# A fused decoder layer on one core: the output projection by pairs of token blocks

## The chip, the cores and the metric

The kernel runs on one core of a Trainium2 chip. The metric is device time in microseconds (us) of one execution. The engines are TensorE (PE, with its weight loads shown apart as PEld), VectorE (DVE), ScalarE (ACT), GpSimd (POOL) and SyncE (SP), which issues the DMAs here.

## The reference, cut to what matters

One decoder layer over 2048 tokens with 1024 channels, all in float32. The input goes through RMSNorm and one input projection into two token mixers of 512 channels each, an S5 scan with GLU and an RG-LRU. Their outputs are normalised, concatenated, projected and added to the residual; then come a SwiGLU feed-forward block and a last RMSNorm.

```python
s5_out  = s5_mixer(u, ...)        # ends in: z = gelu(y); z = z * sigmoid(z @ w_glu + b_glu)
lru_out = rglru_mixer(xr, yr, ...)
mix = concatenate([rms_norm(s5_out, s5_out_g), rms_norm(lru_out, lru_out_g)], axis=-1)
x = x + mix @ w_out               # the output projection, 1024 x 1024
h2 = rms_norm(x, norm2_g)
x = x + (silu(h2 @ w_gate) * (h2 @ w_up)) @ w_down
return rms_norm(x, final_g)
```

The change concerns the GLU and the line with `w_out`, and by its place the start of the gate/up stage that follows.

## The kernel before, in words

Channels lie on the 128 partitions and tokens on the free axis. The 2048 tokens are four blocks of TB = 512 (NB = 4), so that a product fills one PSUM bank (128 x 512 in float32).

**Matrix products in three parts.** Every float32 operand is split into a high part, rounded to the fast float32 format, and a low part, the rest. `mm3` (L193) does three matmuls for each 128 x 128 piece of weights: high x high, high x low, low x high. `Unit` (L168) loads a group of weights in parts of four pieces: the load into `wraw` (L181, six buffers), the cast to `whi` on ScalarE (L187, four buffers) and the subtraction to `wlo` on VectorE or GpSimd (L188, four buffers). A group of the output projection (128 output channels, eight pieces) is two such parts, and takes 24 matmuls for a block of tokens.

**The stages around the change.** `in_tb` (L593) does the input projection and the RG-LRU of one block. The S5 scan runs in two halves of the tokens (L840, blocks 0 and 1, then 2 and 3), eight steps each; its second half runs beside the GLU and the projection of the first two blocks. `glu_tb` (L859) does the GLU of a block: it loads z (L866, `zload`) and the RG-LRU output (`lload`), applies GELU, splits z (`zsplit`, L884), multiplies with `w_glu` (96 matmuls for two blocks), applies the sigmoid and the product (L908), sums squares, and `finish` (L242) makes the factor `rs`. `mix` (L914) then norms each of eight chunks: `norm_split` (L280) does nf on VectorE (L282), the cast (L283) and the subtraction on VectorE or GpSimd (L284). The result goes to `pair(b)` (L856): the pieces aH and aL for blocks 0 and 2, the tiles actH and actL for blocks 1 and 3. `out_tb` (L924) does the projection of a block: for each of eight groups m of weights the 24 matmuls into one of two banks named acc (L142), the addition of the residual (L940, `xc`), the square and its sum, and the store to `x1d` (L942). `finish` then writes the factor of the second RMSNorm to `r2d`.

**The gate/up stage behind it.** `x_first` (L1055) prepares its operands for blocks 0 and 1 in four steps of one chunk k: two loads of `x1d` and one of `r2d` into three tiles `hx` (L1025, L1027), the norm (L1031), sums of the blocks (L1039 to L1042, into four tiles `ht`), and the splits to xh and xl (L995, L996). Each product (L1156) sums over all four chunks. `weights` (L1095) loads and combines the weights.

**Memory.** `open_d1` (L969) closes the pools of the earlier stages (sQ with aH and aL, sL, sS) and opens the pool of the gate/up stage over them. A tile waits for the last reader of what lay there before. In the compiled kernel before, the three hx lie over aH and aL (bytes 47,712 to 60,000 of each partition: aH chunks 0 to 3, aL chunks 4 and 5), the four ht over aH chunks 4 to 7, and the xh and xl of chunk 0 of three products over the rest of aL; the others lie over the pools sL and sS.

**Order.** Each step is put into a plan with a due time (`at`, L64), counted from PT = 0.65 for each piece of weights. The steps are emitted by due time; the compiler then orders each engine's instructions by a simulated schedule in which the emitted order is the priority and an instruction whose inputs or tiles are not ready lets later ones pass. The order of the stages is a list: GLU of 1, projection of 0, projection of 1, GLU of 2, GLU of 3, projection of 2, projection of 3 (L953; GLU of 0 stands in the input stage, L951). tC is the planned end of the projection; `open_d1` is due at tC - 64 PT + 4 and `x_first` at tC - 64 PT + 12 (L1404, L1406), which is the planned begin of block 3's projection.

Of the kernel before, what the change touches and what calls it, by code (L numbers as in the profile page):

```python
# [17 lines left out]
SEQ, DM, TB = 2048, 1024, 512  # L18
NB = SEQ // TB
# [8 lines left out]
PT = 0.65  # L28
# [31 lines left out]
class Plan:  # L60
# [3 lines left out]
    def at(self, t, fn):  # L64
        self.ev.append((t, len(self.ev), fn))
# [14 lines left out]
def build(tc, nc, I, O, ctx):  # L80
    pl = Plan()
    at = pl.at
    PE, DV, AC, GP, SP = nc.tensor, nc.vector, nc.scalar, nc.gpsimd, nc.sync
# [33 lines left out]
    def dram(name, shape):  # L117
        return tc.dram_tile(list(shape), F32, name=name)
# [7 lines left out]
    r2d = dram("r2d", (SEQ,))  # L126
# [6 lines left out]
    xT, out = I["xT"], O  # L133
# [8 lines left out]
    def acc():  # L142
        return PS.tile([128, TB], F32, tag="acc", name="acc", bufs=2)

    last = {}

    def act(**kw):

        ins = AC.activation(**kw)
        ins = getattr(ins, "ins", ins)  # L150
        if "i" in last:
            tc.add_manual_dep(ins, last["i"].name, NOSYNC, reason="tables")
        last["i"] = ins

    def aux(tag, bufs=1):
        return PS.tile([128, TB], F32, tag=tag, name=tag, bufs=bufs)

    def t2(tag, pool=None):
        return (pool or A).tile([128, TB], F32, tag=tag, name=tag, bufs=2)

    def tp():
        return S["p"]

    def r_(ap):
        return ap.bitcast(R)
# [35 lines left out]
    def chunks_of(t):  # L201
        return lambda k: t[:, k, :]
# [67 lines left out]
    def load_chunk(src, b, k, pool=A, tag="xc", bufs=4):  # L270
        t = pool.tile([128, TB], F32, tag=tag, name=tag, bufs=bufs)
        SP.dma_start(t, src[k * 128:(k + 1) * 128, b * TB:(b + 1) * TB])
        return t
# [292 lines left out]
    def lt(tag, shape=(128, 2, TB), dt=F32, bufs=1):  # L566
        return pL.tile(list(shape), dt, tag=tag, name=tag, bufs=bufs)
# [157 lines left out]
    T = 0.0  # L725
    tin = []
    for b in range(NB):
        tin.append(T)
        T = in_tb(b, T)
# [11 lines left out]
    def bt(tag, shape=(128, 2, NS), bufs=1):  # L741
        return S["p"].tile(list(shape), F32, tag=tag, name=tag, bufs=bufs)
# [109 lines left out]
    C = {}  # L852

    t2s = tP1 + 1.0

    def pair(b):  # L856
        return (areaH, areaL) if b % 2 == 0 else (chunks_of(actH), chunks_of(actL))

    def glu_tb(b, t0):  # L859
        cur = C[b] = {}  # L860

        def zload():
            z = cur["z"] = S["z"] if b % 2 == 0 else lt("wg", (128, 4, TB))
            o = CB * (b % 2)
            for j in range(4):
                SP.dma_start(z[:, j].rearrange("p (t c) -> p t c", t=CT),  # L866
                             zb[b // 2, :, 8 * j:8 * j + 8, :, o:o + CB].rearrange("t g h c -> (g h) t c"))

        def lload():
            cur["rl"] = lt("xq", (128, TB))  # L870
            cur["l"] = [lt("r", bufs=2) for _ in range(2)]
            SP.dma_start(cur["rl"], rld[b].unsqueeze(0).to_broadcast([128, TB]))
            for h in range(2):
                SP.dma_start(cur["l"][h], lrud[256 * h:256 * h + 256, b * TB:(b + 1) * TB].rearrange("(j p) t -> p j t", j=2))

        def zgelu():
            act(out=cur["z"], in_=cur["z"], func=AF.Gelu_apprx_tanh)

        def zsplit():
            zh, zl = pair(b)  # L880
            z = cur["z"]
            for j in range(4):
                AC.copy(r_(zh(j)), z[:, j, :])
                DV.tensor_tensor(out=r_(zl(j)), in0=z[:, j, :], in1=zh(j), op=ALU.subtract)  # L884

        at(tin[3] + 35.0 if b < 2 else t0 - 12.0, zload)
        at(max(t0 - 1.5, tin[3] + 50.0), lload)
        at(tin[3] + 36.5 + 0.1 * b if b < 2 else t0 - 5.0, zgelu)
        at(t0 - 5.0 if b == 0 else max(t0 - 5.0, t2s), zsplit)
        cur["ss"] = SumSq(4, "sumg", 2)  # L890
        for uu in range(2):
            t = t0 + uu * 8 * PT
            u = Unit(t, I["w_glu"][uu], 8, GP if uu else DV)

            def prod(uu=uu, u=u):
                for i in range(2):
                    cur["ps", 2 * uu + i] = acc()
                    mm3(cur["ps", 2 * uu + i], u, [(4 * i + k, k) for k in range(4)],
                        *pair(b), True, True)

            at(t, prod)

            def post(uu=uu):
                for i in range(2):
                    m = 2 * uu + i
                    sg = t2("sg", tp())
                    act(out=sg, in_=cur.pop(("ps", m)), func=AF.Sigmoid, bias=pc("bglu", m))
                    DV.tensor_tensor(out=cur["z"][:, m, :], in0=sg, in1=cur["z"][:, m, :], op=ALU.mult)  # L908
                    cur["ss"].add(cur["z"][:, m, :])

            at(t + 8 * PT + 0.5, post)
        t = t0 + 16 * PT

        def mix(k):  # L914
            src, rs = (cur["z"][:, k, :], cur["rs"]) if k < 4 else (cur["l"][k // 2 - 2][:, k % 2, :], cur["rl"])
            norm_split(k, src, pc("gm", k), rs, *pair(b), eng=GP if k % 2 else DV)

        for i, k in enumerate((4, 5, 6, 7)):
            at(max(t0 + 6.0, t2s) + 0.5 * i, lambda k=k: mix(k))
        at(t + 6.0, lambda: cur.__setitem__("rs", cur["ss"].finish()))  # L920
        for k in range(4):
            at(t + 7.0 + 0.5 * k, lambda k=k: mix(k))

    def out_tb(b, t0):  # L924
        cur = C[b]
        ss = SumSq(8, dv=b == NB - 1)
        for m in range(8):
            t = t0 + m * 8 * PT
            u = Unit(t, I["w_out"][m], 8, GP if m % 3 == 1 else DV)

            def prod(m=m, u=u):
                cur["o", m] = acc()
                mm3(cur["o", m], u, [(k, k) for k in range(8)], *pair(b), True, True)

            at(t - 5, lambda m=m: cur.__setitem__(("x", m), load_chunk(xT, b, m)))
            at(t, prod)

            def post(m=m):
                xc = cur.pop(("x", m))
                DV.tensor_tensor(out=xc, in0=cur.pop(("o", m)), in1=xc, op=ALU.add)  # L940
                ss.add(xc)
                SP.dma_start(x1d[128 * m:128 * m + 128, b * TB:(b + 1) * TB], xc)  # L942

            at(t + 8 * PT + 0.5, post)

        def fin():
            ss.finish(r2d[b * TB:(b + 1) * TB])

        at(t0 + 64 * PT + 4.0, fin)

    glu_tb(0, tin[3] + 64 * PT + 5.3)  # L951
    T = tP1 + 16 * PT
    for kind, b in (("g", 1), ("o", 0), ("o", 1), ("g", 2), ("g", 3), ("o", 2), ("o", 3)):  # L953
        if kind == "g":
            glu_tb(b, T)
            T += 16 * PT
        else:
            out_tb(b, T)
            T += 64 * PT
    tC = T  # L960


# [431 lines left out]
    T = tC  # L1394
    gt = {}
# [103 lines left out]
```

## Time and profile before

| | |
|---|---|
| Median of 3 runs | 2208.16 us (2206.6 to 2210.63) |
| Profiled execution | 2207.93 us, span 2206.2 us |
| Instructions | 26,290 |
| Mean granted TensorE clock | 0.949 |
| Matmuls | 8,632 |
| Packets of the main DMA queue | 251,616; 384.69 MB |

The span runs from the first to the last instruction. Busy times of PE come from pipelined matmuls and can overlap, so idle time is read from windows and waits. A wait is put down to what came last before it. "<-" stands between what is written and what is read, or between who waits and whom it waits for; names are those of the program, with L and the line.

### The profile page before, as it was taken

Reading aid. Unit: us, or ns where it says so; the run is one execution under the profiler, and the core shown is the slowest. Engines: PE = TensorE matmul, PEld = TensorE weight load, DVE = VectorE, ACT = ScalarE, POOL = GpSimd, SP = SyncE. Lnnn points to the kernel's source line nnn. Section 1 sums busy time; section 2 is a strip of 40 time slices with the busy share of each in tenths; the row PEclk is TensorE's granted clock in tenths of the full one; section 3 lists DMA queues with packets and bytes.
Section 4 is the critical chain, followed back from the end, with each engine's and each line's share of the span. In section 5 each row is a group of like instructions: output and inputs, shape, how many; then the busy total and the mean of one; then the engine's idle time right before and its main releaser. Section 6 shows DMA issues by size and latency. Waiting matters only on the chain.

```text
span 2206.2 us, 26290 instructions
## 1 busy us (share of the span) xinstructions
PE 1988.3 (90%) x8632; PEld 1582.2 (72%) x8632; DVE 1335.3 (61%) x1975; ACT 812.1 (37%) x1336; POOL 1114.2 (51%) x904
## 2 busy tenths in 40 slices
PE   7668888878988978799999989999999999999996
PEld 5546666656766856577777767777777788888885
DVE  9998868759957397444444474444444535554744
ACT  4433644364344333223233253233232333333331
POOL 3768556649755377654554561231322326644442
PEclk9868999989898988899999999999999999999998
DMA  6244795573763687744444474443443568854733
GB/s 203 86 130 135 196 224 163 180 174 122 234 203 110 206 276 243 257 154 151 149 155 142 151 254 138 134 148 125 145 137 125 171 214 316 301 163 144 247 101 100
DMA packets 251754, 386.37 MB, mean 175 GB/s; under 512 B 59328, under 2 KB 81120, under 8 KB 251616
## 3 DMA queue, kind: packets, MB, share of 16 engines
q1 hardware_dynamic: 251616, 384.69, 55.5%
q8 instruction: 68, 1.11, 0.2%
q14 instruction: 70, 0.57, 0.1%
HBM read 267.92 MB, written 116.67 MB: 174 GB/s over the span
## 4 chain that ended last, share of the span: by engine, by line
PE 63%; DVE 16%; DMA 8%; POOL 5%; issue 4%; ACT 2%; SPq 1%; POOLq 0%; DVEq 0%; ACTq 0%
PE acc L1156 9%; PE gt L1156 9%; PE y L1156 9%; PE acc L198 6%; PE y L1296 5%; PE v L1156 5%; PE acc L1296 5%; PE gt L1296 5%; PE nm L1156 4%; PE nm L1296 2%; PE v L1296 2%; DVE wlo L188 2%; POOL s_s L824 2%; DMA xq<-xT 2%; DVE xh L633 1%
## 5 line engine op out<-in xcount | busy, mean ns | idle before, releaser
L1169 POOL TENSOR_TENSOR t<-t 128x512 f32<-128x512 f32 x66 | 100.6, 1525 | 343.8 <-DVE t L1195 242.2
L198 PE MATMUL acc<-actH,whi 128*128 128x512 f32 x528 | 219.5, 418 | 55.6 <-DVE gy L682 14.0
L995 ACT CAST whi<-ws 128x512 fp32r<-128x512 f32 x176 | 109.1, 620 | 343.1 <-PE gt L1156 91.8
L198 PE MATMUL acc<-actL,whi 128*128 128x512 f32 x528 | 219.7, 417 | 12.9 <-DVE actL L277 12.9
L198 PE MATMUL acc<-actH,wlo 128*128 128x512 f32 x528 | 217.5, 412 | 0.0
L996 DVE TENSOR_TENSOR wlo<-ws,whi 128x512 fp32r<-128x512 f32 x176 | 145.1, 825 | 67.3 <-ACT whi L995 65.3
L996 DVE TENSOR_TENSOR wlo<-ht,whi 128x512 fp32r<-128x512 f32 x112 | 106.0, 949 | 120.6 <-ACT whi L995 120.5
L198 PEld LDWEIGHTS acc<-actH,whi 128*128 128x128 f32 x528 | 105.7, 200 | 87.2 <-issue 35.1
L995 ACT CAST whi<-ht 128x512 fp32r<-128x512 f32 x154 | 95.0, 618 | 168.9 <-PE nm L1296 73.4
L1156 PE MATMUL y<-xh,whi 128*128 128x512 f32 x308 | 124.8, 405 | 16.9 <-ACT t L1188 12.0
L187 ACT CAST whi<-wraw 128x512 fp32r<-128x512 f32 x176 | 106.1, 613 | 86.5 <-PE acc L198 66.2
L996 POOL TENSOR_TENSOR wlo<-ht,whi 128x512 fp32r<-128x512 f32 x42 | 56.7, 1349 | 160.4 <-ACT whi L995 160.3
L198 PEld LDWEIGHTS acc<-actL,whi 128*128 128x128 f32 x528 | 105.6, 200 | 40.9 <-DVE actL L277 19.3
L1156 PE MATMUL acc<-xh,wlo 128*128 128x512 f32 x308 | 124.0, 403 | 8.4 <-DVE wlo L996 8.4
L1156 PE MATMUL acc<-xh,whi 128*128 128x512 f32 x308 | 124.6, 404 | 4.3 <-ACT xh L995 2.3
L1156 PE MATMUL y<-xh,wlo 128*128 128x512 f32 x308 | 123.4, 401 | 5.1 <-DVE wlo L996 5.1
L1156 PE MATMUL y<-xl,whi 128*128 128x512 f32 x308 | 123.9, 402 | 3.7 <-DVE xl L996 3.7
L188 POOL TENSOR_TENSOR wlo<-wraw,whi 128x512 fp32r<-128x512 f32 x64 | 93.9, 1470 | 64.2 <-ACT whi L187 63.7
L188 DVE TENSOR_TENSOR wlo<-wraw,whi 128x512 fp32r<-128x512 f32 x112 | 101.9, 914 | 39.1 <-ACT whi L187 32.3
L1156 PE MATMUL acc<-xl,whi 128*128 128x512 f32 x308 | 123.7, 402 | 1.4 <-DVE xl L996 1.4
L198 PEld LDWEIGHTS acc<-actH,wlo 128*128 128x128 f32 x528 | 106.3, 201 | 23.3 <-issue 0.9
L1156 PE MATMUL gt<-xh,whi 128*128 128x512 f32 x308 | 122.2, 397 | 0.5 <-DVE t L1193 0.5
(421 smaller groups left out, 5522.0 us busy)
## 6 DMA issues: line engine op xcount, KB each, us to landing
td<-t SPq DMA_DIRECT2D x154, 256.0 KB, 2.2
ht<-td SPq DMA_DIRECT2D x154, 256.0 KB, 2.8
wraw<-w_down SPq DMA_DIRECT2D x99, 256.0 KB, 4.5
wraw<-w_in SPq DMA_DIRECT2D x96, 256.0 KB, 3.9
scd<-ws SPq DMA_DIRECT2D x88, 256.0 KB, 2.2
ws<-scd SPq DMA_DIRECT2D x88, 256.0 KB, 2.6
wraw<-w_out SPq DMA_DIRECT2D x64, 256.0 KB, 3.5
xc<-xT SPq DMA_DIRECT2D x56, 256.0 KB, 4.3
```

Source lines behind the costliest of these rows:

```text
L187: AC.copy(hi[:, :n, :], raw)
L188: eng.tensor_tensor(out=lo[:, :n, :], in0=raw, in1=hi[:, :n, :].bitcast(F32), op=ALU.subtract)
L198: PE.matmul(ps, lhsT=part[w][:, kw % 4, :], rhs=r_(x(kx)), start=first and i == 0 and j == 0, stop=last and i == n - 1 and j == 2)
L633: DV.scalar_tensor_tensor(out=xh[:, i, :], in0=xr[:, 1 + k:1 + k + TB], scalar=pc("cw", 4 * k + m), in1=xh[:, i, :], op0=ALU.mult, op1=ALU ...
L824: GP.tensor_tensor(out=sv[64 * ri:64 * ri + 64, gl, :, 1:], in0=a[p], in1=c[p], op=op)
L995: AC.copy(hi, raw)
L996: eng.tensor_tensor(out=lo, in0=raw, in1=hi.bitcast(F32), op=ALU.subtract)
L1156: PE.matmul(ps, lhsT=a[:, k, :], rhs=x, start=j in FIRST and k == 0 and i == 0, stop=k == 3 and i == 2, skip_group_check=True)
L1169: (DV if q == 0 else GP).tensor_tensor(out=g, in0=c, in1=g, op=ALU.mult)
L1296: PE.matmul(BK[p][i], lhsT=a[:, i, :], rhs=x, start=j in FIRST and s == 0 and v == 0, stop=s == NSL - 1 and v == 2, skip_group_check=True)
```

## The change

`glu_tb` can be told when to mix (`tm`), and the buffers of the later blocks are parted: odd blocks load the RG-LRU output into `T` and its factor into `ig` in place of `r` and `xq`, and the split z of blocks 2 and 3 goes to a tile in the place of `u8` (the S5 scan's input) in place of `pair(b)`. `out_tb` is replaced by `out_pair`, which uses each group of weights for two blocks. The products of a pair take turns over four PSUM banks, two named acc and two named gt. For blocks 0 and 1 the order of the 16 products is: groups 0 and 1 of block 0, groups 0 and 1 of block 1, groups 2 to 5 alternating between the blocks, then the GLUs of blocks 2 and 3, then groups 6 and 7 of block 0 and of block 1. For blocks 2 and 3 it is: groups 0 and 1 of block 2, of block 3, then groups 2 to 7 alternating. The sums of squares of blocks 2 and 3 are both added on VectorE (before: only those of block 3). The planned length of the stage and the due times of the gate/up stage stay as they were.

```diff
-    def glu_tb(b, t0):
+    def glu_tb(b, t0, tm=None):
...
-            cur["rl"] = lt("xq", (128, TB))
-            cur["l"] = [lt("r", bufs=2) for _ in range(2)]
+            cur["rl"] = lt("xq" if b % 2 == 0 else "ig", (128, TB))
+            cur["l"] = [lt("rT"[b % 2], bufs=2) for _ in range(2)]
...
+        def zpair():
+            if b < 2:
+                return pair(b)
+            if "zhl" not in cur:
+                zz = bt("u8", (128, 2, 4, TB))
+                cur["zhl"] = tuple((lambda k, i=i: zz[:, i, k, :]) for i in range(2))
+            return cur["zhl"]
+
         def zsplit():
-            zh, zl = pair(b)
+            zh, zl = zpair()
...
-                        *pair(b), True, True)
+                        *zpair(), True, True)
...
+        tm = t + 7.0 if tm is None else tm
...
-            at(max(t0 + 6.0, t2s) + 0.5 * i, lambda k=k: mix(k))
+            at((max(t0 + 6.0, t2s) if b < 2 else tm - 2.0) + 0.5 * i, lambda k=k: mix(k))
...
-            at(t + 7.0 + 0.5 * k, lambda k=k: mix(k))
-
-    def out_tb(b, t0):
-        cur = C[b]
-        ss = SumSq(8, dv=b == NB - 1)
-        for m in range(8):
-            t = t0 + m * 8 * PT
-            u = Unit(t, I["w_out"][m], 8, GP if m % 3 == 1 else DV)
-
-            def prod(m=m, u=u):
-                cur["o", m] = acc()
+            at(tm + 0.5 * k, lambda k=k: mix(k))
+
+    def out_bank():
+        n = last["bank"] = last.get("bank", -1) + 1
+        return acc() if n % 4 < 2 else aux("gt", 2)
+
+    def out_pair(b0, t0):
+        sums = {b: SumSq(8, ("sum", "sumh")[b % 2], dv=b >= NB - 2) for b in (b0, b0 + 1)}
+        blocks = (b0, b0 + 1)
+        order = [(m, b) for b in blocks for m in (0, 1)]
+        order += [(m, b) for m in range(2, 6 if b0 == 0 else 8) for b in blocks]
+        if b0 == 0:
+            order += [(m, b) for b in blocks for m in (6, 7)]
+        units = {}
+        for n, (m, b) in enumerate(order):
+            cur = C[b]
+            t = t0 + n * 8 * PT + (32 * PT if b0 == 0 and n >= 12 else 0)
+            if m not in units:
+                units[m] = Unit(t, I["w_out"][m], 8, GP if m % 3 == 1 else DV)
+
+            def prod(m=m, b=b, cur=cur, u=units[m]):
+                cur["o", m] = out_bank()
                 mm3(cur["o", m], u, [(k, k) for k in range(8)], *pair(b), True, True)
...
+            if m == 7:
+                at(t + 8 * PT + 4.0, lambda b=b: sums[b].finish(r2d[b * TB:(b + 1) * TB]))
 
     glu_tb(0, tin[3] + 64 * PT + 5.3)
     T = tP1 + 16 * PT
-    for kind, b in (("g", 1), ("o", 0), ("o", 1), ("g", 2), ("g", 3), ("o", 2), ("o", 3)):
-        if kind == "g":
-            glu_tb(b, T)
-            T += 16 * PT
-        else:
-            out_tb(b, T)
-            T += 64 * PT
+    glu_tb(1, T)
+    T += 16 * PT
+    out_pair(0, T)
+
+    tg = T + 96 * PT
+    glu_tb(2, tg, T + (128 + 16 + 1) * PT)
+    glu_tb(3, tg + 16 * PT, T + (128 + 32 + 1) * PT)
+    T += 128 * PT + 32 * PT
+    out_pair(2, T)
+    T += 128 * PT
     tC = T
```

More of the change, by code (lines that the diff above doesn't have):

```diff
@@ L933, in prod, with post @@
                 mm3(cur["o", m], u, [(k, k) for k in range(8)], *pair(b), True, True)
-            at(t - 5, lambda m=m: cur.__setitem__(("x", m), load_chunk(xT, b, m)))
-            at(t, prod)
-            def post(m=m):
+            def post(m=m, b=b, cur=cur):
                 xc = cur.pop(("x", m))
                 DV.tensor_tensor(out=xc, in0=cur.pop(("o", m)), in1=xc, op=ALU.add)
-                ss.add(xc)
+                sums[b].add(xc)
                 SP.dma_start(x1d[128 * m:128 * m + 128, b * TB:(b + 1) * TB], xc)
+            at(t - 5, lambda m=m, b=b, cur=cur: cur.__setitem__(("x", m), load_chunk(xT, b, m)))
@@ L944, in out_tb @@
+            at(t, prod)
             at(t + 8 * PT + 0.5, post)
-        def fin():
-            ss.finish(r2d[b * TB:(b + 1) * TB])
-        at(t0 + 64 * PT + 4.0, fin)
+            if m == 7:
+                at(t + 8 * PT + 4.0, lambda b=b: sums[b].finish(r2d[b * TB:(b + 1) * TB]))
     glu_tb(0, tin[3] + 64 * PT + 5.3)
     T = tP1 + 16 * PT
-    for kind, b in (("g", 1), ("o", 0), ("o", 1), ("g", 2), ("g", 3), ("o", 2), ("o", 3)):
-        if kind == "g":
-            glu_tb(b, T)
-            T += 16 * PT
-        else:
-            out_tb(b, T)
-            T += 64 * PT
+    glu_tb(1, T)
```

## The prediction

> **What bounds the kernel now.** I read the page first, then the busy time of each engine stage by stage, the waits, and last the instructions in order of time around the output projection.
>
> ```profile
> PE 1988.3 (90%) x8632; PEld 1582.2 (72%) x8632; DVE 1335.3 (61%) x1975; ACT 812.1 (37%) x1336; POOL 1114.2 (51%) x904
> ```
>
> Over the span TensorE is the bound, and the change takes no large matmul away. So a gain can only be TensorE idle time that goes away in the stretch that the change touches. By windows (length, then busy time of PE, PEld, DVE, ACT, POOL, then granted clock, DMA share, GB/s):
>
> ```profile
> 541.30:567.00 25.70, 21.48 (x81) 15.19 (x82) 25.24 (x43) 7.01 (x14) 20.39 (x30) 0.67 0.52 159
> 567.00:604.00 37.00, 35.86 (x193) 28.66 (x192) 33.55 (x55) 11.82 (x22) 30.70 (x37) 1.00 0.86 251
> 604.00:655.40 51.40, 43.29 (x186) 34.85 (x186) 26.51 (x51) 21.65 (x36) 28.95 (x28) 0.90 0.69 201
> 655.40:719.90 64.50, 54.38 (x231) 43.53 (x232) 42.97 (x71) 30.35 (x53) 31.54 (x23) 0.89 0.38 115
> 719.90:759.60 39.70, 39.70 (x172) 32.19 (x171) 16.09 (x23) 16.42 (x27) 17.43 (x13) 1.00 0.61 183
> 759.60:819.60 60.00, 50.71 (x218) 40.03 (x217) 50.74 (x57) 22.51 (x40) 37.95 (x23) 0.96 0.86 282
> 819.60:846.80 27.20, 14.56 (x39) 8.59 (x39) 20.47 (x31) 11.36 (x21) 15.20 (x10) 0.63 0.76 245
> ```
>
> The rows are: block 0's projection starting while VectorE is full (25.24 of 25.70 us); block 0 going on; its end and block 1; block 1's end with both later GLUs; block 2's projection; block 3's projection; the start of the gate/up stage. The fifth row is the stage as it should be: 172 matmuls in 39.70 us, 0.231 us each, so 5.5 us for the 24 matmuls of one product (one group of weights, one block). The matmul counts of the projection and GLU line alone (L198) in two of these rows tell what the others lose:
>
> ```profile
> 655.40:719.90 64.50, 48.99 (x189) 36.89 (x190) 0.89 0.38 115
> 759.60:819.60 60.00, 44.69 (x193) 35.65 (x192) 0.96 0.86 282
> ```
>
> In the GLU row 189 x 0.231 = 43.7 us of work, and 42 small matmuls at 0.12 (0.95 us for eight, below) 5.0 us, fill 64.5 us: about 16 us are lost. Who TensorE waited for from 541.3 to 719.9 (total, times, longest):
>
> ```profile
> PE acc L198 <- DVE xc L940: 7.2, 5, 2.2
> PE acc L198 <- ACT aH L283: 6.5, 3, 4.4
> PE y L834 <- DMA mo<-md: 2.7, 1, 2.7
> 767.20 0.95 PE L246 MATMUL nm<-ones,sum 128*128 128x1 f32 x8
> ```
>
> The first is the wait for one of two PSUM banks, the second the GLU's way to the mixed activations. These are what the change can win.
>
> **The change part by part.** *Weights once for two blocks.* The loads fall from 64 to 32, the casts by 32, the subtractions by 20 on VectorE and 12 on GpSimd (m of 1, 4, 7 go there, two parts each, four blocks before and two after).
>
> ```profile
> wraw<-w_out SPq DMA_DIRECT2D x64, 256.0 KB, 3.5
> L187 ACT CAST whi<-wraw 128x512 fp32r<-128x512 f32 x176 | 106.1, 613 | 86.5 <-PE acc L198 66.2
> L188 DVE TENSOR_TENSOR wlo<-wraw,whi 128x512 fp32r<-128x512 f32 x112 | 101.9, 914 | 39.1 <-ACT whi L187 32.3
> L188 POOL TENSOR_TENSOR wlo<-wraw,whi 128x512 fp32r<-128x512 f32 x64 | 93.9, 1470 | 64.2 <-ACT whi L187 63.7
> ```
>
> That is 32 x 0.613 = 19.6 us of ScalarE, 20 x 0.914 = 18.3 us of VectorE, 12 x 1.470 = 17.6 us of GpSimd and 8 MB of DMA. In the block 2 row VectorE is busy 16 of 39.7 us and TensorE never waits, so there this is worth nothing; it counts only where VectorE is full, 541 to 604.
>
> *The order of the first four products.* They become block 0 with groups 0 and 1, then block 1 with groups 0 and 1. whi and wlo have four buffers, two for each group, so groups 0 and 1 hold all four until block 1 has used them: group 2 cannot be split, and block 0 cannot run ahead as it does now. When are the activations ready?
>
> ```profile
> 565.02 0.69 DVE L940 TENSOR_TENSOR xc<-acc,xc 128x512 f32<-128x512 f32 x1 [0.35 <-PE acc L198]
> 567.56 0.69 DVE L940 TENSOR_TENSOR xc<-acc,xc 128x512 f32<-128x512 f32 x1
> 584.06 1.38 DVE L282 SCALAR_TENSOR_TENSOR nf<-wg,par,rs 128x512 f32<-128x512 f32 x2
> 595.65 1.27 POOL L284 TENSOR_TENSOR actL<-nf,actH 128x512 fp32r<-128x512 f32 x1
> ```
>
> Block 0's first two products are evacuated by 567.6. The first mixed chunk of block 1 is begun at 584.06 and chunk 3 is split at 595.65 + 1.27 = 596.9. Now TensorE fills this time with block 0's groups 2 to 5 (the 567 to 604 row: 193 matmuls, 35.86 us busy of 37). After the change it waits, apart from a few small matmuls of the S5 scan. From 596.9 the five remaining chunks of two products are 30 x 0.231 = 6.9 us, to 603.8. VectorE drops some seven operations of 0.69 us from this time (two evacuations, five weight subtractions), so it may be 599; I take 601.5. That moves a stall rather than work: four of block 0's products must be made up later.
>
> *From there to the end of the projection.* 28 products and the two GLUs (96 matmuls) are 768 x 0.231 = 177.4 us. Small matmuls: the 42 in each of the third and fourth rows (186 less 144 of L198, 231 less 189), 84 x 0.12 = 10 us. What remains of the stalls: bank waits go (four banks); the DMA wait of 2.7 stays; the chain sigmoid, sum of squares, rs, mix is covered by four products (22 us) for block 2 and by two products of block 2 for block 3, against which stand eight mixed chunks in 11 us. I take 8 us, half of the 16 lost now, between 2 and 16. The later GLUs start at 601.5 + 44 + 4 = 649.5, and the z that they need is split from 650.38 on today:
>
> ```profile
> 650.38 3.76 DVE L884 TENSOR_TENSOR aL<-zA,aH 128x512 fp32r<-128x512 f32 x4 [6.38 <-ACT aH L883]
> 819.66 0.68 DVE L940 TENSOR_TENSOR xc<-acc,xc 128x512 f32<-128x512 f32 x1
> ```
>
> so this fits with a few us of wait, inside the 8. The end E of the projection is 601.5 + 177.4 + 10 + 8 = 797 (between 788 and 807); now it is 819.7. **Gain at that point: 23 us.** Some of it is only that the gate/up preparation no longer runs beside block 3, which today stretches block 3's 44.6 us of matmuls (193 x 0.231) to 60 us.
>
> *What moves behind the projection without standing in the diff.* The gate/up stage's first tiles (three hx, four ht, the splits of chunk 0) lie in the memory of block 0's and 2's activations, aH and aL. SP issues them like this:
>
> ```profile
> 759.44 0.39 PE L198 MATMUL acc<-aH,wlo 128*128 128x512 f32 x1
> 759.29 0.90 SPq L1025 DMA_DIRECT2D hx<-x1d  x2
> 760.96 0.72 SPq L1027 DMA_DIRECT2D hx<-r2d  x1
> SPq L1025 <- PE acc L198: 0.4, 1, 0.4
> ```
>
> The first hx load goes out as block 2's last matmul does, and has waited for a matmul of the projection: the fourth row. Today block 2 ends 60 us before block 3, and the preparation runs in that time. After the change block 2's last product is the last but one, so hx can be loaded only 5.5 us before E. Its pace, by the first norm operation of each of four steps and of the step after them:
>
> ```profile
> 769.87 1.28 DVE L1031 SCALAR_TENSOR_TENSOR hx<-hx,par 128x1024 f32<-128x1024 f32 x1 [3.22 <-DMA hx<-r2d]
> 787.76 1.28 DVE L1031 SCALAR_TENSOR_TENSOR hx<-hx,par 128x1024 f32<-128x1024 f32 x1
> 806.63 2.31 DVE L1031 SCALAR_TENSOR_TENSOR hx<-hx,par 128x1024 f32<-128x1024 f32 x1
> 827.92 1.28 DVE L1031 SCALAR_TENSOR_TENSOR hx<-hx,par 128x1024 f32<-128x1024 f32 x1
> 842.47 1.85 DVE L1031 SCALAR_TENSOR_TENSOR hx<-hx,par 128x1024 f32<-128x1024 f32 x1 [0.65 <-DMA hx<-r2d]
> ```
>
> Three buffers carry one step, so the steps are a chain: load, norm, sums, release, load. Beside block 3 a step takes 17.9 to 21.3 us; the last, with the projection gone, 14.6. Every product of gate/up needs all four chunks, so TensorE runs steadily only at 846.8, 18.9 after the fourth norm. After the change: first norm at E + 3 (10.3 after block 2's end today; 8.5 taken, with less traffic), three steps of 14 (12 to 14.6), and 17 (15 to 18.9) to the steady state: E + 62, between E + 54 and E + 67. At E = 797 that is 859 against 846.8, **12 us later**. The few gate/up matmuls that stand before 846.8 today (among the 25 that the 759.6 row has beyond L198's 193, and the 39 of the row after it) are done by then in both. Behind it the stage runs as before, so the shift reaches the end. The same in idle time: today 87 us lie between block 2's end and the steady state, with block 3 under them; afterwards 67, with one product under them.
>
> What else moves: block 1's and 3's rl and r come into other buffers, off the path; block 2's seven additions of squares go from GpSimd to VectorE, 7 times about the 0.69 us of the L940 row, where VectorE has room; SP issues 32 loads less. I price these at nothing; were VectorE full there too, 5 us.
>
> *A rule weighed.* The clock row says 0.67 and 0.63 in the two stretches with idle time and 1.00 where TensorE is full. The Trainium skill (TensorE: Matmul & The Clock Gate, section "Part 1: The HAM clock gate") says that after an idle window of about 3.4 us the array runs at half rate until a busy window has passed. By it the new wait of 567 to 587 would cost about 1.7 us more, an estimate from that page, and the sum would be 14 instead of 12. I leave it out, since my 8 us of stalls hold such losses; the trace agrees with the direction.
>
> The Trainium skill (Perfetto Trace Analysis, "Matmuls") also says that independent groups should rotate through banks, so that evacuation overlaps. By it the 7.2 us of bank waits all go; the sum has them gone already, and here the rule speaks only for the change.
>
> **The rivals.** *Faster.* The projection's gain outweighs the late start: block 1's mix comes early because VectorE is relieved, E = 788, and a preparation step alone takes 11 us with 15 behind: 788 + 3 + 33 + 15 = 839, 8 us earlier, 2200. For it: VectorE full at 541 to 604 and 23 us of gain at E. Against: the only undisturbed step took 14.6. It decides at E + offset = 846.8, so at an offset of 58.8 when E is 788. If the scheduler finds the preparation room before block 2's end, it is 797 + 27 = 824, 2185; the fourth row of that fence speaks against it.
>
> *No change.* E = 790 and offset 57: 847. For it: both numbers lie inside my bounds.
>
> *Much slower.* Nothing won from 541 to 720 (E = 807) and offset 67: 874, 27 us later, 2235. For it: the eight mixed chunks in 11 us, and the wait for block 1 with an idle clock.
>
> *It does not do what it says*: the weights' halving is certain by the code; that it is not what bounds is part of the forecast.
>
> **How the numbers follow.** The profiled execution took 2207.93 us (span 2206.2), the median of the runs is 2208.16; the sum is against the first: 2207.93 + 12 = 2220. About 0.2% (4.4 us) is what a measurement can tell from no change. Chances: the forecast (5 to 20 us slower) 0.54, much slower 0.12, no change 0.14, faster 0.20, of which 0.05 for the preparation not waiting. So slower 0.66, same 0.14, faster 0.20. The range reaches from 2200, the faster rival's own time, to 2235, the much slower one's; the forecast's own is 2213 to 2228.
>
> **What would show it.** Right: an idle stretch of TensorE of 15 to 20 us behind block 0's first two products, ended by block 1's mix; no wait for L940 on the banks; GLU and mix with less than 10 us lost; the first hx load within 10 us of the last projection matmul; TensorE mostly idle for some 40 to 50 us after that. Wrong: hx loads 30 us or more ahead of the end of the projection, steps of 11 us or less, or block 1's first product right behind block 0's second.

## The result and the profile after

The changed kernel takes 2233.7 us (median of four runs, 2228.36 to 2236.22), the kernel before 2207.38 beside it (2204.5 to 2210.63): a ratio of 1.0116, 95% interval 1.0091 to 1.0140. It is 26 us slower. The forecast, 12 us slower at 2220, had the direction and the place of the loss, and less than half of its size. The profiled execution is the slowest of the four, 2236.22 us with a span of 2234.4.

The page's first row for the changed kernel:

```profile
PE 1986.8 (89%) x8632; PEld 1577.3 (71%) x8632; DVE 1314.7 (59%) x1962; ACT 796.9 (36%) x1304; POOL 1084.6 (49%) x885
```

ScalarE is busy 15.2 us less, VectorE 20.6, GpSimd 29.6, and TensorE as long as before. Work went, as the parts said, and the time did not fall with it: it is in TensorE's idle stretches. The windows of the changed kernel, in the columns of the prediction:

```profile
541.30:567.00 25.70, 19.44 (x82) 12.76 (x80) 25.60 (x42) 8.23 (x16) 22.45 (x28) 0.80 0.53 153
567.00:596.70 29.70, 20.80 (x108) 16.87 (x110) 23.29 (x53) 7.73 (x15) 24.48 (x43) 0.83 0.71 202
596.70:647.00 50.30, 49.03 (x240) 40.23 (x237) 17.33 (x30) 17.78 (x27) 21.72 (x21) 1.00 0.66 186
647.00:701.50 54.50, 52.13 (x223) 41.38 (x221) 29.40 (x47) 26.10 (x43) 23.73 (x18) 0.94 0.32 96
701.50:734.00 32.50, 27.62 (x116) 19.92 (x116) 26.12 (x49) 12.11 (x21) 12.28 (x9) 0.95 0.31 94
734.00:801.50 67.50, 67.50 (x296) 54.61 (x295) 21.78 (x37) 14.08 (x23) 5.17 (x4) 1.00 0.50 154
801.50:828.50 27.00, 7.28 (x25) 4.18 (x23) 23.39 (x36) 5.63 (x10) 18.44 (x11) 0.55 0.64 224
828.50:872.90 44.40, 18.48 (x39) 9.09 (x39) 31.32 (x29) 16.64 (x28) 24.15 (x15) 0.58 0.60 191
```

The second row is the new wait behind block 0's first two products. The sixth is the projection at its best, with little beside it: VectorE 21.78 of 67.50 us, GpSimd 5.17. The last two are the bill: 71.4 us in which TensorE is busy for 25.8. The chain of preparation steps in the changed kernel, with the load before it, the last addition of the residual, the norm of each chunk and the first matmul of the steady part:

```profile
791.88 2.89 SPq L1049 DMA_DIRECT2D hx<-x1d  x2
801.55 0.69 DVE L962 TENSOR_TENSOR xc<-gt,xc 128x512 f32<-128x512 f32 x1 [3.31 <-DMA rd<-w_up]
802.15 3.48 DVE L1055 SCALAR_TENSOR_TENSOR hx<-hx,par 128x1024 f32<-128x1024 f32 x2
828.53 2.48 DVE L1055 SCALAR_TENSOR_TENSOR hx<-hx,par 128x1024 f32<-128x1024 f32 x2
841.52 2.48 DVE L1055 SCALAR_TENSOR_TENSOR hx<-hx,par 128x1024 f32<-128x1024 f32 x2 [4.07 <-DMA hx<-r2d]
854.66 2.48 DVE L1055 SCALAR_TENSOR_TENSOR hx<-hx,par 128x1024 f32<-128x1024 f32 x2 [4.23 <-DMA hx<-r2d]
872.92 0.80 PE L1180 MATMUL acc<-xh,whi 128*128 128x512 f32 x1 [1.01 <-DVE t L1217]
```

Steps of 26.4, 13.0 and 13.1 us, then 18.3 to the steady part at 872.9, which was at 846.8 before: 26.1 us, nearly the whole of the 28.3 between the two profiled executions. That it stays so is seen far behind, by the first and last start of one kind of matmul of the down projection, in the kernel before and in the changed one:

```profile
L1296 PE MATMUL y<-whi,wdh x154: 390/393/404, 1743.6 to 2150.7; 128*128 128x512 f32 x154
```

```profile
L1320 PE MATMUL y<-whi,wdh x154: 390/393/503, 1769.1 to 2178.9; 128*128 128x512 f32 x154
```

The first start is 25.5 us later, the last 28.2. I use the first start below as the mark of how late a kernel is when the gate/up stage is over.

Why is the first step twice as long as the next? GpSimd, VectorE and SyncE of the changed kernel between the first two norms:

```profile
802.74 1.82 POOL L1137 TENSOR_TENSOR ws<-wraw,rd 128x512 f32<-128x512 f32 x1 [21.46 <-DMA rd<-w_gate]
...
806.72 1.71 POOL L1137 TENSOR_TENSOR ws<-ws,wraw 128x512 f32<-128x512 f32 x1
...
811.76 1.79 POOL L1137 TENSOR_TENSOR ws<-wraw,ws 128x512 f32<-128x512 f32 x1
...
815.25 1.78 POOL L1066 TENSOR_TENSOR ht<-hx,ht 128x512 f32<-128x512 f32 x1
816.99 1.70 POOL L1137 TENSOR_TENSOR ws<-ws,wraw 128x512 f32<-128x512 f32 x1
820.00 1.26 POOL L1137 TENSOR_TENSOR ws<-wraw 128x512 f32<-128x512 f32 x1 [1.30 <-DVE nv L218]
```

```profile
807.24 1.75 DVE L1020 TENSOR_TENSOR xl<-hx,xh 128x512 fp32r<-128x512 f32 x1
...
819.24 0.68 DVE L1020 TENSOR_TENSOR wlo<-ws,whi 128x512 fp32r<-128x512 f32 x1
...
826.26 0.16 DVE L210 TENSOR_SCALAR nv<-nm 128x4 f32<-128x4 f32 x1 [2.98 <-PE nm L246]
```

```profile
817.05 0.33 SPq L1051 DMA_DIRECT2D hx<-r2d  x1
```

Seven sums of gate and up weights (`wsum`, L1137) stand on GpSimd between 802.7 and 821.3, among the four operations that the chunk needs. The chunk's last sum (L1066) comes only at 815.25, the buffer is free then, and the next `r2d` load leaves at 817.05. And VectorE has the reciprocal roots of blocks 2 and 3 in its order (`rsqrt`, L210 to L218): the second chain waits for TensorE until 826.26, and the next norm is queued behind it until 828.53.

### The profile page after: what moved, and what is told of

It reads as the page before. It is cut to its first block, busy times and chain, and to the rows that moved or that the text cites. A ratio compares the mean times of both kernels' runs of the same rounds, so it can differ in the third digit from the quotient of the medians.

```text
span 2234.4 us, 26078 instructions
## 1 busy us (share of the span) xinstructions
PE 1986.8 (89%) x8632; PEld 1577.3 (71%) x8632; DVE 1314.7 (59%) x1962; ACT 796.9 (36%) x1304; POOL 1084.6 (49%) x885
## 4 chain that ended last, share of the span: by engine, by line
PE 65%; DVE 17%; DMA 7%; POOL 4%; issue 4%; ACT 2%; SPq 1%; POOLq 0%; DVEq 0%; ACTq 0%
PE acc L1180 9%; PE gt L1180 9%; PE y L1180 8%; PE acc L198 7%; PE v L1180 5%; PE y L1320 4%; PE nm L1180 4%; PE acc L1320 4%; PE gt L1320 4%; PE gt L198 3%; PE nm L1320 2%; PE v L1320 2%; POOL s_s L824 1%; DVE wlo L188 1%; DMA ht<-xcd 1%
## 5 line engine op out<-in xcount | busy, mean ns | idle before, releaser
L198 PE MATMUL acc<-actH,whi 128*128 128x512 f32 x424 | 177.2, 421 | 54.8 <-DVE gy L682 20.9
L198 PE MATMUL acc<-actL,whi 128*128 128x512 f32 x424 | 177.8, 420 | 15.6 <-DVE actL L277 15.5
L198 PE MATMUL acc<-actH,wlo 128*128 128x512 f32 x424 | 175.7, 415 | 0.0
L198 PEld LDWEIGHTS acc<-actH,whi 128*128 128x128 f32 x424 | 85.7, 202 | 79.4 <-issue 35.2
L188 POOL TENSOR_TENSOR wlo<-wraw,whi 128x512 fp32r<-128x512 f32 x52 | 75.5, 1454 | 113.4 <-ACT whi L187 112.9
L1180 PE MATMUL gt<-xh,wlo 128*128 128x512 f32 x308 | 121.2, 393 | 0.0
L1180 PE MATMUL gt<-xl,whi 128*128 128x512 f32 x308 | 121.1, 393 | 0.0
L1019 ACT CAST whi<-wraw 128x512 fp32r<-128x512 f32 x88 | 54.5, 620 | 175.3 <-PE y L1180 63.2
L187 ACT CAST whi<-wraw 128x512 fp32r<-128x512 f32 x144 | 87.0, 614 | 83.0 <-PE acc L198 56.2
```

What stands on the lines that cost most here:

```text
L187: AC.copy(hi[:, :n, :], raw)
L188: eng.tensor_tensor(out=lo[:, :n, :], in0=raw, in1=hi[:, :n, :].bitcast(F32), op=ALU.subtract)
L198: PE.matmul(ps, lhsT=part[w][:, kw % 4, :], rhs=r_(x(kx)), start=first and i == 0 and j == 0, stop=last and i == n - 1 and j == 2)
L1019: AC.copy(hi, raw)
L1180: PE.matmul(ps, lhsT=a[:, k, :], rhs=x, start=j in FIRST and k == 0 and i == 0, stop=k == 3 and i == 2, skip_group_check=True)
```

## The experiments

Seventeen runs, told in the order of the questions. A ratio is to the kernel before on the same chip.

**Is it the late start of the preparation?** Blocks 2 and 3 are taken one after the other again, each with its own loads; the first pair and the GLU inside it stay.

```diff
+        if b0:
+            order = [(m, b) for b in blocks for m in range(8)]
...
-            if m not in units:
+            key = (m, b) if b0 else m
+            if key not in units:
```

> Blocks 2 and 3 are projected one after the other again (each with its own loads of the weights, still over four banks); blocks 0 and 1 stay a pair, with the GLUs inside. Theory, memory: the loss comes from the gate/up tiles that lie over block 2's activations, which the second pair keeps alive to its end. Then the first hx load goes out some 40 us before the end of the projection again, the first part's gain stays, and the time is about 2199 us (2193 to 2205), 8 us under the kernel before and 35 under the changed one. Rival, the rest of the change: the late GLU inside the pair, the four banks or the additions on VectorE cost the time; then it stays at 2225 to 2236.

2202.55 us, ratio 0.9982 (0.9971 to 0.9993), where the theory had it. The first load and the first norm of this kernel:

```profile
756.63 0.86 SPq L1052 DMA_DIRECT2D hx<-x1d  x2
766.96 2.48 DVE L1058 SCALAR_TENSOR_TENSOR hx<-hx,par 128x1024 f32<-128x1024 f32 x2 [3.04 <-DMA hx<-r2d]
```

35 us earlier than in the changed kernel, and the loss is gone: the second pair makes the 26 us and some more (31 between the medians). The ratio also prices the first pair with the GLU inside: about 4 us of gain. The other half of the cut, the first pair apart and the second kept (the same lines with the condition turned round, and the GLUs behind the projections):

> The other half alone: blocks 2 and 3 stay a pair, blocks 0 and 1 are projected one after the other and the later GLUs come behind them, as before the change. Theory, memory: the late start of the gate/up preparation stays and the first part's gain is lost, so the time is 2236 to 2245 us, 3 to 10 over the changed kernel. Rival, the wait for block 1 at the head of the first pair costs more than the GLUs inside it give: the time is under the changed kernel's by 5 us or more, 2228 or less.

2228.11 us, ratio 1.0102 (1.0086 to 1.0117). The theory of a first half that gains here too was missed, and the rival isn't shown either: against the changed kernel's 1.0116 (1.0091 to 1.0140) the intervals overlap. With the second pair in place nothing that the first half wins is seen.

**Is it the bytes under hx?** The prediction put the late load down to the memory: hx lies over aH and aL. So the pool with aH and aL was moved away from under hx, to the other side of the memory, in the changed kernel and, as a control, in the kernel before. The order in which the pools are closed follows.

```diff
-    Q = sQ.enter_context(tc.tile_pool(name="Q", bufs=1, reuse_waits="tile"))
+    Q = sQ.enter_context(tc.tile_pool(name="Q", bufs=1, side="right", reuse_waits="tile"))
```

> The changed kernel with one word moved: the pool of aH and aL is opened at the other end of the memory, so that of the gate/up tiles only the splits of chunk 3, the sums of weights (ws) and one rd lie over them; hx, ht and chunks 0 to 2 lie over tiles that are free once block 3 is mixed. No work is changed. Theory, memory: the first hx load goes out by 740 us, three of the four preparation steps are done before the projection ends at about 801, TensorE runs steadily 25 to 35 us after that instead of 72, and the time is 2188 to 2200 us. Rival, the preparation is bound by VectorE and GpSimd and not by memory: 2222 to 2236 us.

> The kernel before with the same move of the pool, as a control. Theory, memory: the preparation can start when block 3 is mixed, some 30 us before block 2 ends, so this kernel gains too, but less, because its preparation runs beside 44 us of projection already: 2190 to 2203 us. Rival, placement matters only where a pair is kept alive: 2204 to 2211, no change.

2230.72 us, ratio 1.0118 (1.0103 to 1.0133), and 2206.85, ratio 1.0001 (0.9991 to 1.0011): nothing. The theory of the bytes fell. The first load of the changed kernel with the move:

```profile
788.17 0.92 SPq L1049 DMA_DIRECT2D hx<-x1d  x2
```

In this kernel the load waits for no matmul any more, since no byte of it is block 2's; in the compiled order it still stands behind five of the projection's stores that were emitted after it. Some tiles of the pool D1 lie over block 2's data, and the whole pool, hx with it, is placed in the schedule behind the last reader there. The next run tests that: the same tiles in two pools, the second with only the tiles that must lie over aH and aL (the last chunk's xh and xl, one pair more, and `ws`). The move of the pool Q stays in.

```diff
         sL.close()
-        sQ.close()
         sS.close()
         D["1"] = sD1.enter_context(tc.tile_pool(name="D1", bufs=1, reuse_waits="tile"))
+        sQ.close()
+        D["b"] = sDb.enter_context(tc.tile_pool(name="Db", bufs=1, reuse_waits="tile"))
...
-        return D["2" if j in LATE else "1"].tile([128, TB], dt, tag=tag, name=name or tag, bufs=1)
+        return D["2" if j in LATE else "b" if k == 3 or (j, k) == (4, 2) else "1"].tile([128, TB], dt, tag=tag, name=name or tag, bufs=1)
```

> The changed kernel with its tiles where they were needed split over two pools: what lies over the GLU and scan buffers opens by itself when block 3 is mixed, and only the last chunk's x tiles and the ws buffers lie over the areas that hold block 2. Theory (the chunk preparation is late because the one pool that holds it cannot open before block 2's last product, whichever bytes its first tile lies on): the hx loads come about 85 us earlier, near 705 instead of 792, four chunk preparations lie beside the projection, and the gate products run steadily within 25 us of the projection's end: 2165 to 2205 us. Rival (the loads are late for their place in SyncE's order or the preparation cannot run beside the projection, so the pool is no cause): 2222 us or more.

2189.14 us, ratio 0.9925 (0.9901 to 0.9948). The first loads and norms of this kernel:

```profile
724.43 0.86 SPq L1050 DMA_DIRECT2D hx<-x1d  x2
743.82 0.37 SPq L1052 DMA_DIRECT2D hx<-r2d  x1
```

```profile
748.50 2.48 DVE L1056 SCALAR_TENSOR_TENSOR hx<-hx,par 128x1024 f32<-128x1024 f32 x2 [3.25 <-DMA hx<-r2d]
...
794.12 2.48 DVE L1056 SCALAR_TENSOR_TENSOR hx<-hx,par 128x1024 f32<-128x1024 f32 x2 [3.74 <-DMA x1d<-xc]
```

All four norms now lie before the projection's end; the mark in the down stage comes at 1722.9, 46 us before the changed kernel's. The load came 67 us earlier rather than 85, and the time is where the theory put it. Against the run before it only the boundary of the pool has moved, so the boundary was the cause. The same split in the kernel before:

> The kernel before with the same split. The theory expects a gain here too, since its preparation also starts only at block 2's last product, but a smaller one, 10 to 25 us (2181 to 2197), and a time 10 to 25 us above the changed kernel with the split, because its projection ends some 19 us later. The rival that two blocks a weight group bring nothing expects both split kernels within 5 us of each other.

2184.3 us, ratio 0.9904 (0.9879 to 0.9930). Here the theory was missed: the kernel before with the split is not 10 to 25 us behind the two-block kernel with it, but level or a little ahead. The last projection matmul starts at 799.7 in the two-block kernel and 818.0 in the other, and that lead was worth nothing at the end. The last addition of the residual, in the two-block kernel with the split and in the kernel before with it, shows where most of the lead is lost:

```profile
816.44 0.68 DVE L962 TENSOR_TENSOR xc<-gt,xc 128x512 f32<-128x512 f32 x1
```

```profile
818.44 0.69 DVE L940 TENSOR_TENSOR xc<-acc,xc 128x512 f32<-128x512 f32 x1 [3.71 <-PE acc L198]
```

On VectorE the lead is 2 us: in the two-block kernel the last product is taken up there 16.8 us after the start of its last matmul, behind the preparation's work.

**What makes the first step 26 us?** The sums and the chains were taken away one at a time. For the sums, in `wsum`:

```diff
-            GP.tensor_tensor(out=sm[j], in0=a, in1=c, op=op)
+            if uid[1] == 0:
+                sm[j] = a
+            else:
+                GP.tensor_tensor(out=sm[j], in0=a, in1=c, op=op)
```

> The changed kernel with the eight first weight sums of gate and up (slab 0, 1.75 us each on GpSimd) left out, a raw weight block standing in for each sum. Theory (the first chunk step of 26.4 us is long because these sums hold GpSimd and slow VectorE beside it): the step falls to 15 to 18 us, and the time by 8 to 12 us to 2222 to 2226. Rival (the two reciprocal-root chains set the step): under 3 us.

2216.15 us, ratio 1.0040 (1.0026 to 1.0054), 17.5 us less. Its first two norms:

```profile
797.96 2.47 DVE L1055 SCALAR_TENSOR_TENSOR hx<-hx,par 128x1024 f32<-128x1024 f32 x2
812.12 2.48 DVE L1055 SCALAR_TENSOR_TENSOR hx<-hx,par 128x1024 f32<-128x1024 f32 x2 [1.58 <-DMA hx<-r2d]
```

A step of 14.2: all of the excess is gone. The time fell by 17.5 us where 8 to 12 were expected. TensorE runs steadily from 859.98, 12.9 us earlier, and in the 140 us behind that it does 543 matmuls where the changed kernel does 497, so the rest is won there; by what, no run here shows. For the chains, `finish` of blocks 2 and 3 stores a row of the sums at once:

```diff
+            if self.dv:
+                row = P.tile([4, 128], F32, tag="row", name="row", bufs=2)
+                AC.copy(row, self.s[0:4, 0:128])
+                SP.dma_start(dst.rearrange("(i t) -> i t", i=4), row)
+                return
```

> The changed kernel with the reciprocal roots of blocks 2 and 3 left out (a row of the sums is stored in their place). Theory (GpSimd's weight sums set the first chunk step of 26.4 us, the chains fill a wait that is there anyway): under 4 us, 2229 to 2234. Rival (the chains on VectorE, with the second one's wait for TensorE, set the step): the step falls to 14 to 18 us and the time by 8 to 12 us to 2222 to 2226.

2226.47 us, ratio 1.0094 (1.0071 to 1.0116): a step of 20.2 (norms at 800.88 and 821.05) and 7 us, between the theory and the rival. Both explanations had a part. The chains can also be moved with nothing left out: the column sums stay, the chain is queued on VectorE behind the first gate unit's evacuation.

```diff
+        def total(self):
+            ps = aux("nm")
+            ...
+            self.v = P.tile([128, 4], F32, tag="sv", name="sv", bufs=2)
+            DV.tensor_copy(out=self.v, in_=ps[:, 0:4])
...
+                with tc.issue_after(getattr(last["e"], "ins", last["e"])):
+                    y = rsqrt(self.v, 128 * self.n)
```

> The changed kernel with the two reciprocal-root chains behind the first gate unit and nothing left out. If the chains cost what leaving them out gave (7 us, the first chunk step 20.2 instead of 26.4): 2224 to 2230 us. If they only fill a wait that GpSimd sets: 2231 or more.

2219.35 us, ratio 1.0054 (1.0038 to 1.0070), 14.4 us less, below the range of both. The first two norms:

```profile
803.24 3.51 DVE L1067 SCALAR_TENSOR_TENSOR hx<-hx,par 128x1024 f32<-128x1024 f32 x2 [0.47 <-DMA hx<-r2d]
823.33 2.48 DVE L1067 SCALAR_TENSOR_TENSOR hx<-hx,par 128x1024 f32<-128x1024 f32 x2 [2.55 <-DMA hx<-r2d]
```

A step of 20.1: the norm now waits for its load, no longer for a chain. But the mark at the down stage is only 8.2 us earlier (1760.9), so the rest comes from behind it. There the matmuls ran faster than in any kernel without this edit: 219 and 220 in its first two 50 us rather than 216 to 217. Before that was followed up, the two together:

> The changed kernel with the eight first weight sums of gate and up left out and the two reciprocal-root chains moved behind the first gate unit. If the sums (17.5 us by the run without them) and the chains (14.4 us by the run that moved them) are two separate costs: 2199 to 2207 us, with a first chunk step near 13. If both are one cost, the same wait counted twice: 2211 or more.

2214.05 us, ratio 1.0024 (1.0011 to 1.0038): beyond the sums alone the chains give 2 us. They are one wait counted twice: without the sums the second norm waits for its load (the 1.58 us above), and no longer for a chain.

The edit for the late roots also puts two tiles of 16 bytes into the first pool. By them every tile of three later pools lies 64 bytes higher, among them D1 with the operands of the gate/up and the down stage (the tiles of the pools sS and D2 stay where they were). Those two tiles alone, set to zero and never read:

```diff
+            if m == 7 and b0:
+                at(t + 8 * PT + 3.0, lambda: DV.memset(P.tile([128, 4], F32, tag="sv", name="sv", bufs=2), 0.0))
```

> The changed kernel with nothing moved but two unused tiles of 16 bytes set to zero, so that every tile of the later pools lies 64 bytes higher, as in the runs with late roots. Those ran the down stage's matmuls at 219 to 220 in 50 us where all others ran 216 to 217. If the bytes are the cause: 219 to 220 here too, and 4 to 7 us less, 2227 to 2230, so that of the late roots' 14.4 us some 5 belong to the bytes. If it is the order of the instructions: 216 to 217, and no change in time.

> The kernel before with the same two unused tiles. If the bytes are the cause: 219 to 220 matmuls in 50 us of the down stage and 4 to 7 us less than before, 2200 to 2203. If not: 216 to 217, and no change.

2231.45 us, ratio 1.0098 (1.0081 to 1.0114), and for the kernel before 2201.46, ratio 0.9972 (0.9960 to 0.9983). The second 50 us of the down stage in the changed kernel and in the changed kernel with the two tiles (length, PE busy and count, clock, DMA share, GB/s):

```profile
1819.10:1869.10 50.00, 50.00 (x217) 1.00 0.82 283
```

```profile
1824.50:1874.50 50.00, 50.00 (x220) 1.00 0.83 286
```

That is 0.227 us for a matmul rather than 0.230, at the same clock. The down stage of the changed kernel and of the kernel before, both with the two tiles:

```profile
L1322 PE MATMUL y<-whi,wdh x154: 388/388/397, 1774.5 to 2176.4; 128*128 128x512 f32 x154
```

```profile
L1298 PE MATMUL y<-whi,wdh x154: 388/394/398, 1749.6 to 2151.7; 128*128 128x512 f32 x154
```

From the first of these starts to the last there are 401.9 and 402.1 us, where the same two kernels without the tiles take 409.8 and 407.1. Over all nineteen kernels it is 401.5 to 402.8 us in the eight with the tiles, and 407.1 to 409.8 in the eleven without. The two settings to zero run at 1.0 us, and every other instruction of the changed kernel keeps its place in the compiled order: the bytes do it. In the time of the whole kernel the 6 us of the kernel before are clear, while the changed kernel's 2231.45 lies between the two expectations, and its interval overlaps the one without the tiles. If the stage's 5.4 us are taken off the late roots' 14.4, some 9 belong to the chains; and the 2 us of the late roots without the sums, above, are no more than the bytes give.

**Are two blocks a weight group worth anything when the preparation is early?** Both split kernels with late roots:

> The split-pool version of the changed kernel, with the reciprocal roots of blocks 2 and 3 queued on VectorE behind the first gate unit's evacuation (their column sums are taken at the old place). Theory (in the split version the shorter projection, which ends near 800 against 818, is lost again to these two chains: 7.7 us of waits of TensorE and a clock near 0.6 of full between 805 and 833): the loss goes, 2172 to 2182 us, at least 3 us below the kernel before with the same two edits. Rival (two blocks a weight group bring nothing once the preparation is covered, since VectorE and the queue are then the bound): 2183 to 2190, level with or above the kernel before with the same edits.

> The kernel before with the split pools and block 3's reciprocal root behind the first gate unit. Only one chain stood there, with 2.4 us of waits: both the theory and the rival expect little, 2180 to 2185 us.

2184.22 us, ratio 0.9899 (0.9881 to 0.9917), and 2184.7, ratio 0.9895 (0.9879 to 0.9911): level, the rival. The 5 us that the first is under the two-block kernel with the split alone are no more than the bytes give. With both edits and the eight sums left out of both:

> The changed kernel with split pools and late roots, and the eight first weight sums left out. Theory (the two-block projection is worth its earlier end, 800 against 818, as soon as nothing else is late): 8 us or more below the kernel before with the same edits, 2160 to 2174 us. Rival (what is left of VectorE's and GpSimd's work before the steady state sets it, whenever the projection ends): within 5 us of it, 2172 to 2184.

> The kernel before with split pools and late roots, and the same eight weight sums left out. Theory and rival both expect a little under the version with the sums: 2175 to 2184 us.

2177.41 us, ratio 0.9858 (0.9842 to 0.9874), and 2185.32, ratio 0.9890 (0.9870 to 0.9909). The second is a little above its expectation: in the kernel before, leaving out the sums gave nothing. Between the medians lie 7.9 us, just short of the least that the theory asked for (8 us or more); the intervals of the ratios touch, but the times of the first (2176.84 to 2179.24) all lie under those of the second (2180.54 to 2189.95). From 760 to 801 the split two-block kernel with late roots, and the split kernel before with late roots:

```profile
760.00:801.00 41.00, 39.06 (x172) 31.75 (x170) 34.46 (x33) 12.02 (x21) 21.30 (x12) 1.00 0.77 233
```

```profile
760.00:801.00 41.00, 35.37 (x152) 27.55 (x151) 37.31 (x44) 17.40 (x31) 29.18 (x17) 0.96 0.89 283
```

VectorE is busy 34 and 37 of 41 us in the two: it is nearly full, whichever way the weights are taken. That fits the rival, and so does the late last addition in the two-block kernel with the split; the runs without the sums point the other way, by less than half of the 18 us. How much two blocks for a weight group are worth when nothing else is late is not settled.

**Four banks or two?** The changed kernel with `return acc()` for every product:

> The changed kernel with its output products in two PSUM banks instead of four. If the banks carry what the kernel before waited for them (7.2 us in 32 products): the projection ends 3 to 7 us later and the time is 2236 to 2241. If two blocks a weight group alone remove that wait: within 2 us of 2234.

2230.48 us, ratio 1.0099 (1.0079 to 1.0119), and the last residual addition at 801.23 against 801.55: the second case, though 3.5 us under 2234 and not within 2; the interval overlaps the changed kernel's. So it is not the two extra banks that removed the bank waits: they bring nothing here, and the rest of the change is enough. The Trainium skill's rule that the prediction named (Perfetto Trace Analysis, "Matmuls") is met in both: no wait for the residual addition (L962) is left among TensorE's.

## Where the prediction was right and where it failed

*Work taken away is worth nothing by itself.* Right: the three engines are relieved, TensorE's busy time is the same, and the time did not fall.

*The wait for block 1.* Right as a place, too long by 5 us. The norm of the first mixed chunk came at 576.09, 8 us sooner than before the change, and block 1's first two products were evacuated here, the second 4.8 us ahead of the 601.5 taken:

```profile
594.87 0.68 DVE L962 TENSOR_TENSOR xc<-gt,xc 128x512 f32<-128x512 f32 x1
596.68 0.68 DVE L962 TENSOR_TENSOR xc<-gt,xc 128x512 f32<-128x512 f32 x1
```

The sign, an idle stretch of 15 to 20 us, was too strong. TensorE's longest wait there is 7.9 us and ends at 573.4, when block 1's factor is made; then matmuls of the S5 scan run until the first matmul of block 1's products at 579.8.

*The end of the projection, E = 797.* Nearly right: 801.5, inside 788 to 807. The 4.8 us won above are more than spent behind it: from 596.7 to 801.5 there are 204.8 us for 187.4 of matmuls, so 17.4 us were lost where "I take 8 us" stood, a little over the upper bound of 16. TensorE is idle for only 8.5 of them. The rest comes from the 768 large matmuls, which took 187.5 us in place of 177.4.

*The first hx load just before E.* Right in time, 791.88, and right in what it does, by the run with the second pair apart. But the reason given, that hx lies over aH and aL, was too narrow: taken off those bytes it came only 4 us earlier (788.17), and with the pool split 67. The place of the first tile is not what decides; the pool is.

*"Three steps of 14 (12 to 14.6)".* **This is the step that failed.** First norm at E + 0.6 (3 forecast), steps of 26.4, 13.0 and 13.1, then 18.3 (17 forecast): 71.4 against 62. The offset brought 9.4 us of the missing 14, E the other 4.6. All of the 9.4 and more is the first step, 12.4 over its value. The price of 14 came from the one step of the kernel before without the projection beside it, 14.6 from 827.92 to 842.47, and that step held one weight sum of the first eight. The other seven stood in the two steps before it, which I had read as slowed by the projection: in the kernel before

```profile
799.75 1.74 POOL L1113 TENSOR_TENSOR ws<-wraw,rd 128x512 f32<-128x512 f32 x1
...
821.50 1.66 POOL L1113 TENSOR_TENSOR ws<-wraw 128x512 f32<-128x512 f32 x1 [0.63 <-DVE wlo L996]
...
836.89 1.66 POOL L1113 TENSOR_TENSOR ws<-wraw,ws 128x512 f32<-128x512 f32 x1 [0.63 <-DVE wlo L996]
```

are the first and the last of the seven, spread over two steps, and the eighth. `rd` lies in the same pool as hx and moves with it, so all seven came to stand in one step. Block 2's root moved too: before, its chain began at 772.3 and block 3's at 825.7, in two different steps, and after the change both stand in that one. The prediction listed hx, ht and the splits as what moves with the memory, and not the sums and the roots. Without the sums the step is 14.2, the value that was forecast.

*The rival "much slower" (2235)* named the right size for another reason: it asked for E = 807 and an offset of 67, with nothing won before.

*The clock.* The prediction left the idle stretch's clock to the stalls. In the last two rows of the windows the granted clock is 0.55 and 0.58, lower than the 0.63 of the kernel before in the same place. The Trainium skill (TensorE: Matmul & The Clock Gate, "Part 1: The HAM clock gate") has the array at half rate after an idle window, and the rows agree. What it cost was not measured apart.

## What to carry to other kernels

When an edit moves the release of a buffer, list every first use in the pool that opens behind it, on every engine, and not only the tile whose wait the trace shows: weight loads and their sums move with it. Take the price of a step from a row in which the same operations stand in it. And ask first whether the next stage can begin without the buffer: the split pool, which leaves the projection alone, brought 22 us in the kernel before, and the change to the projection by itself lost 26.

## What the runs showed of the hardware

VectorE is slower beside GpSimd: the subtraction of two 128 x 512 tiles takes 0.68 us alone and 1.75 beside a GpSimd sum (the rows at 819.24 and 807.24). The chain's tiny operations can suffer most; one of 0.17 us took 1.24:

```profile
812.34 1.24 DVE L213 TENSOR_SCALAR nv<-nv 128x4 int32<-128x4 int32 x1
813.49 0.68 DVE L1020 TENSOR_TENSOR wlo<-ws,whi 128x512 fp32r<-128x512 f32 x1
...
826.66 0.17 DVE L213 TENSOR_SCALAR nv<-nv 128x4 int32<-128x4 int32 x1
```

The Trainium skill (SBUF — State Buffer, "Who interferes with whom") says that a VectorE instruction with two inputs in SBUF contends with a GpSimd instruction that reads SBUF; the 0.68 and 1.75 us agree. The tiny operation has only one input, and the rows show it waiting too: it ends at 813.58, 0.03 us behind the end of the GpSimd sum begun at 811.76. Not every operation waits: the one after it, at 813.49, took 0.68 us with a GpSimd sum on record beside it. So in this step a sum on GpSimd costs twice, on GpSimd and on VectorE beside it.

I had also not expected that 64 bytes of address change the rate of the down stage's matmuls by 1.4% (217 to 220 in 50 us) at a granted clock of 1.00, and the length of that stage by 5 us or more. The runs show that the bytes are the cause; why, they don't show.
